# Top-2 gate and dispatch: another map from blocks of tokens to partitions

## The chip, the cores and the metric

The kernel runs on one core of one Trainium2 chip. The metric is the device time of one execution in microseconds, as the median of several runs. Before the change three runs took 239.9, 240.08 and 240.19 us, so the median is 240.08 us.

## The reference

For each of 16 x 1024 tokens there are 512 hidden values and 8 router logits. The two largest probabilities of a softmax over the logits are divided by their sum, and the token's hidden row is written twice, once times each of the two weights, the smaller first. Cut to what matters:

```python
probs = np.exp(router_logits - logits_max)
probs = probs / np.sum(probs, axis=-1, keepdims=True)
topk_indices = np.argsort(probs, axis=-1)[..., -k:]          # k = 2
topk_probs = np.take_along_axis(probs, topk_indices, axis=-1)
topk_probs = topk_probs / np.sum(topk_probs, axis=-1, keepdims=True)
x_expanded = x[:, :, np.newaxis, :].repeat(k, axis=2)
return (x_expanded * topk_probs[..., np.newaxis]).astype(np.float32)
```

x has 33.55 MB, the logits 0.52 MB and the output 67.11 MB, all float32. No two tokens depend on each other, so any token may lie in any partition as long as its row, its logits and its output agree.

## The kernel before

The 16,384 tokens are 128 partitions times 128 tokens. They are worked in two groups (`GROUPS = [65, 63]`): the first holds 65 tokens per partition, the second 63. In each group a partition holds a block of consecutive tokens: the view `(p m) d -> p m d` gives partition p the tokens p·m to p·m + m - 1 of the group. A token's row is 2 KiB, so a block is 130 KiB of x and 260 KiB of the output in the first group, 126 and 252 KiB in the second.

A group's rows are loaded into `xs` by a few transfers over all 128 partitions (`LOADS`, line 120: 2, 4, 28 and 31 tokens per partition, then 16, 16 and 31). Behind the second load the two transfers of the logits are issued (lines 125 and 126), and `top2_weights` (lines 22 to 38) finds the two largest logits of every token by a tree of max and min on VectorE; two sigmoids of their difference on ScalarE are the weights `WA`. As the exponentials' sum drops out, no softmax is formed.

Then each group is stored in pieces (`STORES`). A piece of up to 16 tokens per partition is one multiplication on VectorE (line 133), rows and weights broadcast against each other, which writes both copies. It writes into a separate buffer `osp`, or into `xs` itself over rows that are no longer needed. Where a piece goes into `osp` a second time, the multiplication is cut in two, because a part of the buffer comes free earlier. A transfer stores the piece (line 145).

All loads and all stores but the first stand in SyncE's queue, in the order in which the program gives them (`keep_in_program_order`); the first store is issued from ScalarE. SyncE waits in line: a store waits for its multiplication, and the second group's loads wait for the stores that read the buffer they overwrite.

Of the kernel before, what the change touches and what calls it, by code (L numbers as in the profile page):

```python
# [1 line left out]

# [4 lines left out]

F32 = mybir.dt.float32
ALU = mybir.AluOpType
ACTF = mybir.ActivationFunctionType  # L10
P = 128


def top2_weights(nc, WA, dlt, room, logits, E):

    tt = nc.vector.tensor_tensor
    hi, lo, n = None, None, E  # L20
    while n > 1:
        n //= 2
        if hi is None:
            a, b = logits[:, :, 0:n], logits[:, :, n : 2 * n]
            nhi, nlo = room(n), b
            tt(nhi, a, b, op=ALU.max)  # L26
            tt(nlo, a, b, op=ALU.min)  # L27
        else:
            a, b = hi[:, :, 0:n], hi[:, :, n : 2 * n]
            nhi, nlo, tmp = room(n), room(n), room(n)  # L30
            tt(tmp, lo[:, :, 0:n], lo[:, :, n : 2 * n], op=ALU.max)  # L31
            tt(nlo, a, b, op=ALU.min)  # L32
            tt(nlo, nlo, tmp, op=ALU.max)  # L33
            tt(nhi, a, b, op=ALU.max)  # L34
        hi, lo = nhi, nlo
    tt(dlt, hi[:, :, 0], lo[:, :, 0], op=ALU.subtract)  # L36
    nc.scalar.activation(WA[:, :, 0], dlt, ACTF.Sigmoid, scale=-1.0)  # L37
    nc.scalar.activation(WA[:, :, 1], dlt, ACTF.Sigmoid, scale=1.0)  # L38

GROUPS = [65, 63]

LOADS = [[2, 4, 28, 31], [16, 16, 31]]
BASE = [0, 1]

STORES = [
    [(0, 3, "osp", 0), (3, 15, "osp", 3), (18, 16, "xs", 0), (34, 15, "osp", 0), (49, 16, "xs", 33)],
    [(0, 16, "osp", 2), (16, 16, "xs", 0), (32, 15, "osp", 0), (47, 16, "xs", 32)],
]  # L50

L = 18

FREE = [3, 2]


@with_exitstack
def kernel(
    ctx: ExitStack,
    tc: tile.TileContext,  # L60
    x: bass.AP,
    router_logits: bass.AP,
    k: bass.AP,
    out: bass.AP,
):
    nc = tc.nc
    B, S, D = x.shape
    E = router_logits.shape[-1]
    N = B * S
    assert int(k) == 2 and E == 8 and N == P * sum(GROUPS)  # L70
    M = N // P

    x_v, o_v, rl_v = [], [], []
    t0 = 0
    for n in GROUPS:
        t1 = t0 + P * n
        x_v.append(
            x.rearrange("b s d -> (b s) d")[t0:t1].rearrange("(p m) d -> p m d", p=P)
        )
        o_v.append(  # L80
            out.rearrange("b s k d -> (b s) k d")[t0:t1].rearrange(
                "(p m) k d -> p m k d", p=P
            )
        )
        rl_v.append(
            router_logits.rearrange("b s e -> (b s) e")[t0:t1].rearrange(
                "(p m) e -> p m e", p=P
            )
        )
        t0 = t1  # L90

    wpool = ctx.enter_context(tc.tile_pool(name="wpool", bufs=1))
    xs = wpool.tile([P, max(GROUPS), D], F32)
    osp = wpool.tile([P, L, 2, D], F32)
    WA = wpool.tile([P, M, 2], F32)
    dlt = wpool.tile([P, M], F32)


    flat = osp.rearrange("p l k d -> p (l k d)")
    taken = [0]  # L100

    def room(n):
        o = taken[0]
        taken[0] += M * n
        return flat[:, o : o + M * n].rearrange("p (m n) -> p m n", n=n)

    logits = room(E)

    def place(where, at, n):

        if where == "osp":
            return osp[:, at : at + n]
        return xs[:, at : at + 2 * n, :].rearrange("p (r k) d -> p r k d", k=2)

    m0 = 0
    for g, G in enumerate(GROUPS):
        x0, r = BASE[g], 0
        for n in LOADS[g]:
            tc.keep_in_program_order(
                nc.sync.dma_start(xs[:, x0 + r : x0 + r + n, :], x_v[g][:, r : r + n, :])  # L120
            )
            r += n
            if g == 0 and r == 6:
                n0 = GROUPS[0]
                tc.keep_in_program_order(nc.sync.dma_start(logits[:, :n0], rl_v[0]))  # L125
                tc.keep_in_program_order(nc.sync.dma_start(logits[:, n0:], rl_v[1]))  # L126
                top2_weights(nc, WA, dlt, room, logits, E)
        assert r == G
        for r, n, where, at in STORES[g]:
            og = place(where, at, n)  # L130
            again = where == "osp" and at == 0 and r > 0
            for a, b in [(0, FREE[g]), (FREE[g], n)] if again else [(0, n)]:
                nc.vector.tensor_tensor(  # L133
                    og[:, a:b],
                    xs[:, x0 + r + a : x0 + r + b, :]
                    .unsqueeze(2)
                    .to_broadcast([P, b - a, 2, D]),
                    WA[:, m0 + r + a : m0 + r + b, :]
                    .unsqueeze(3)
                    .to_broadcast([P, b - a, 2, D]),  # L140
                    op=ALU.mult,
                )

            queue = nc.scalar if g == r == 0 else nc.sync
            tc.keep_in_program_order(queue.dma_start(o_v[g][:, r : r + n], og))  # L145
        m0 += G


# [1 line left out]
_INS = ['x', 'router_logits', 'k']  # L150
_OUTS = [((16, 1024, 2, 512), 'float32')]

_NUMBERS = {'k': 2}


# [26 lines left out]
```

## Time and profile before

| What | Value |
|---|---|
| median of three runs | 240.08 us |
| span of the profiled execution | 238.1 us |
| time of the profiled execution beside its span | not given by the page; the median is 2.0 us above the span |
| VectorE busy | 141.9 us (60%), 22 instructions |
| data moved | 101.19 MB in 2593 packets |
| mean rate over the span | 425 GB/s |
| share of the 16 DMA engines' time, SyncE's and ScalarE's queues | 97.2% and 1.5% |

The span is the time from the first to the last instruction that the hardware profiler recorded. "Busy" leaves out waiting, and the issuing of transfers. A transfer is cut into packets that 16 DMA engines move; the profile gives the time from its issue to its landing. The chain that ended last is followed back from the last instruction, at each step to what released it. In a table of stretches, a row has the stretch, its length, the busy time of each engine with the number of instructions, the clock of TensorE (which this kernel doesn't use), the DMA engines' mean busy share and the rate.

### The profile page before, as it was taken

How to read it: one execution, taken by the hardware profiler on the slowest of the kernel's cores; microseconds unless marked ns; L12 is line 12 of the kernel's file. 1: busy time of each engine (PE TensorE's matmuls, PEld its weight loads, DVE VectorE, ACT ScalarE, POOL GpSimd, SP SyncE). 2: the span in 40 equal slices, each digit the busy share in tenths (PEclk: the TensorE clock that was granted, in tenths of full speed). 3: DMA queues.
4: the chain of work that ended last, by engine and by line, in shares of the span. 5: the costliest groups of instructions: out<-in, count | busy, mean ns of one | idle time of the engine just before them, and what ended most of it. 6: DMA issues, size and time to landing. Idle time of an engine off the chain costs nothing.

```text
span 238.1 us, 105 instructions
## 1 busy us (share of the span) xinstructions
DVE 141.9 (60%) x22; ACT 1.8 (1%) x3; POOL 0.2 (0%) x4
## 2 busy tenths in 40 slices
DVE  0560499999689999100000799999406999950000
ACT  2000000000000000000000000000000000000000
POOL 0000000000000000000000000000000000000000
DMA  7979998979998999989899999898999989989894
GB/s 249 537 337 526 419 429 376 506 330 495 407 451 363 517 392 434 495 352 528 352 440 440 429 446 491 363 495 374 484 396 418 462 352 506 475 351 517 352 528 176
DMA packets 2593, 101.19 MB, mean 425 GB/s; under 512 B 289, under 2 KB 417, under 8 KB 673
## 3 DMA queue, kind: packets, MB, share of 16 engines
q1 hardware_dynamic: 2448, 99.62, 97.2%
q10 hardware_dynamic: 144, 1.57, 1.5%
q14 instruction: 1, 0.00, 0.0%
HBM read 34.08 MB, written 67.11 MB: 425 GB/s over the span
## 4 chain that ended last, share of the span: by engine, by line
DMA 48%; DVE 40%; SPq 1%; issue 0%; DVEq 0%
DVE osp L133 25%; DMA xs<-in_x_dram 25%; DMA out_dram<-osp 22%; DVE xs L133 14%; SPq L120 0%; SPq L126 0%; SPq L125 0%; SPq L145 0%; DVEq L133 0%
## 5 line engine op out<-in xcount | busy, mean ns | idle before, releaser
L133 DVE TENSOR_TENSOR osp<-xs,WA 128x3072 f32<-128x3072 f32 (+5 forms) x7 | 69.4, 9909 | 61.2 <-DMA xs<-in_x_dram 47.2
L133 DVE TENSOR_TENSOR xs<-xs,WA 128x16384 f32<-128x16384 f32 x4 | 68.9, 17224 | 0.1
L26 DVE TENSOR_TENSOR osp<-osp 128x512 f32<-128x512 f32 x1 | 0.7, 691 | 8.4 <-DMA osp<-in_router_logits_dram 8.4
L37 ACT ACT_TABLE_LOAD x1 | 1.3, 1283 | 0.7 <-PEq L163 0.7
L27 DVE TENSOR_TENSOR osp<-osp 128x512 f32<-128x512 f32 x1 | 0.7, 691 | 0.0
L31 DVE TENSOR_TENSOR osp<-osp 128x256 f32<-128x256 f32 (+1 forms) x2 | 0.7, 350 | 0.0
L32 DVE TENSOR_TENSOR osp<-osp 128x256 f32<-128x256 f32 (+1 forms) x2 | 0.7, 350 | 0.0
L34 DVE TENSOR_TENSOR osp<-osp 128x256 f32<-128x256 f32 (+1 forms) x2 | 0.7, 349 | 0.0
L33 DVE TENSOR_TENSOR osp<-osp 128x256 f32<-128x256 f32 (+1 forms) x2 | 0.7, 348 | 0.0
L37 ACT ACTIVATE WA<-dlt 128x128 f32<-128x128 f32 x1 | 0.3, 314 | 10.3 <-DVE dlt L36 10.3
L36 DVE TENSOR_TENSOR dlt<-osp 128x128 f32<-128x128 f32 x1 | 0.3, 293 | 0.0
L38 ACT ACTIVATE WA<-dlt 128x128 f32<-128x128 f32 x1 | 0.3, 298 | 0.0
L163 POOL MEMSET const-bfloat16-1.0<- 128x1 bf16 x1 | 0.1, 102 | 0.0
L163 POOL MEMSET const-uint8-127<- 128x1 uint8 x1 | 0.1, 101 | 0.0
L163 POOL MEMSET const-float32-0.0<- 128x1 f32 x1 | 0.1, 99 | 0.2 <-issue 0.2
L163 POOL MEMSET const-float32-1.0<- 128x1 f32 x1 | 0.1, 98 | 0.0
## 6 DMA issues: line engine op xcount, KB each, us to landing
out_dram<-osp SPq DMA_DIRECT2D x3, 7680.0 KB, 23.3
xs<-in_x_dram SPq DMA_DIRECT2D x2, 7936.0 KB, 41.3
xs<-in_x_dram SPq DMA_DIRECT2D x2, 4096.0 KB, 40.3
xs<-in_x_dram SPq DMA_DIRECT2D x1, 7168.0 KB, 24.4
out_dram<-osp ACTq DMA_DIRECT2D x1, 1536.0 KB, 26.9
xs<-in_x_dram SPq DMA_DIRECT2D x1, 1024.0 KB, 5.8
xs<-in_x_dram SPq DMA_DIRECT2D x1, 512.0 KB, 3.8
osp<-in_router_logits_dram SPq DMA_DIRECT2D x1, 260.0 KB, 6.0
```

Of the source, the lines that this page charges most:

```text
L26: tt(nhi, a, b, op=ALU.max)
L27: tt(nlo, a, b, op=ALU.min)
L31: tt(tmp, lo[:, :, 0:n], lo[:, :, n : 2 * n], op=ALU.max)
L32: tt(nlo, a, b, op=ALU.min)
L33: tt(nlo, nlo, tmp, op=ALU.max)
L34: tt(nhi, a, b, op=ALU.max)
L36: tt(dlt, hi[:, :, 0], lo[:, :, 0], op=ALU.subtract)
L37: nc.scalar.activation(WA[:, :, 0], dlt, ACTF.Sigmoid, scale=-1.0)
L38: nc.scalar.activation(WA[:, :, 1], dlt, ACTF.Sigmoid, scale=1.0)
L133: nc.vector.tensor_tensor(og[:, a:b], xs[:, x0 + r + a : x0 + r + b, :] .unsqueeze(2) .to_broadcast([P, b - a, 2, D]), WA[:, m0 + r + a : ...
L163: nc = _bacc.Bacc("TRN2", target_bir_lowering=False, num_devices=1)
```

## The change

Loads, logits and stores all go by another map. Each group's 128 blocks are numbered in four quarters of 32: block 32j + a is the a-th of quarter j. Before, block p lay in partition p. After, block 32j + a lies in partition 4a + j, so that four neighbouring partitions hold one block from each quarter, and the next four hold the blocks next to these.

On the DRAM side a transfer is then described by 32 x 4 pieces with two strides, in place of 128 with one; on the partitions' side it is still 128. A piece is as long as before. In the built program every instruction stands where it stood: the order on VectorE, ScalarE and SyncE and the shapes on VectorE are the same, and the 18 transfers differ only in their DRAM side, such as 32 x 4 x 15360 for a store that had 128 x 15360.

```diff
     for n in GROUPS:
         t1 = t0 + P * n
         x_v.append(
-            x.rearrange("b s d -> (b s) d")[t0:t1].rearrange("(p m) d -> p m d", p=P)
+            x.rearrange("b s d -> (b s) d")[t0:t1].rearrange(
+                "(j a m) d -> a j m d", j=4, m=n
+            )
         )
         o_v.append(
             out.rearrange("b s k d -> (b s) k d")[t0:t1].rearrange(
-                "(p m) k d -> p m k d", p=P
+                "(j a m) k d -> a j m k d", j=4, m=n
             )
         )
         rl_v.append(
             router_logits.rearrange("b s e -> (b s) e")[t0:t1].rearrange(
-                "(p m) e -> p m e", p=P
+                "(j a m) e -> a j m e", j=4, m=n
             )
         )
...
-                nc.sync.dma_start(xs[:, x0 + r : x0 + r + n, :], x_v[g][:, r : r + n, :])
+                nc.sync.dma_start(xs[:, x0 + r : x0 + r + n, :], x_v[g][:, :, r : r + n, :])
...
-            tc.keep_in_program_order(queue.dma_start(o_v[g][:, r : r + n], og))
+            tc.keep_in_program_order(queue.dma_start(o_v[g][:, :, r : r + n], og))
```

## The prediction

> **What bounds the kernel now.** I read the page first for who is busy: busy times, the DMA queues, the chain that ended last.
>
> ```profile
> span 238.1 us, 105 instructions
> DVE 141.9 (60%) x22; ACT 1.8 (1%) x3; POOL 0.2 (0%) x4
> DMA packets 2593, 101.19 MB, mean 425 GB/s; under 512 B 289, under 2 KB 417, under 8 KB 673
> ...
> q1 hardware_dynamic: 2448, 99.62, 97.2%
> q10 hardware_dynamic: 144, 1.57, 1.5%
> ...
> HBM read 34.08 MB, written 67.11 MB: 425 GB/s over the span
> ...
> DMA 48%; DVE 40%; SPq 1%; issue 0%; DVEq 0%
> ```
>
> VectorE is busy for 60% of the span, the packets of SyncE's queue (q1) and ScalarE's queue (q10) for 97.2% + 1.5% = 98.7% of what 16 DMA engines have. The chain's 40% of DVE is no counter-evidence: the chain passes through whichever work was late locally, while the transfers never pause. The second view, waits, says the same: VectorE waits for transfers, 47.2 us for loads and 13.5 us for stores to free buffers.
>
> ```profile
> DVE osp L133 <- DMA xs<-in_x_dram: 47.2, 2, 36.4
> DVE osp L133 <- DMA out_dram<-osp: 13.5, 2, 11.1
> ```
>
> The third view cuts the span into stretches (length; busy us of DVE, ACT, POOL; clock; DMA share; GB/s).
>
> ```profile
> core 0: us, DVE busy (x) ACT busy (x) POOL busy (x), PEclk, DMA share, GB/s
> 0.00:4.00 4.00, 0.00 (x0) 1.28 (x1) 0.20 (x4) 1.00 0.57 166
> 4.00:24.00 20.00, 7.18 (x12) 0.51 (x2) 0.00 (x0) 1.00 1.09 458
> 24.00:28.00 4.00, 1.01 (x1) 0.00 (x0) 0.00 (x0) 1.00 0.82 352
> 28.00:154.00 126.00, 87.08 (x7) 0.00 (x0) 0.00 (x0) 1.00 1.01 436
> 154.00:164.00 10.00, 10.00 (x1) 0.00 (x0) 0.00 (x0) 1.00 0.96 413
> 164.00:214.00 50.00, 36.64 (x4) 0.00 (x0) 0.00 (x0) 1.00 0.99 431
> 214.00:234.00 20.00, 0.00 (x0) 0.00 (x0) 0.00 (x0) 1.00 1.00 433
> 234.00:238.10 4.10, 0.00 (x0) 0.00 (x0) 0.00 (x0) 1.00 0.41 176
> 30.00:230.00 200.00, 131.72 (x10) 0.00 (x0) 0.00 (x0) 1.00 1.00 433
> ```
>
> A share above 1 (1.09) shows that a packet is booked whole where it begins, so only long stretches are exact. From 30 to 230 us the rate is 433 GB/s with all 16 engines full. It is 433 in 214:234, where only stores run and VectorE is idle, and 436 in 28:154, where loads, stores and VectorE overlap. A rate that does not care for direction or for neighbours looks like a limit of the engines themselves, not of the memory behind them. So the time is bytes over rate plus ends: 101.19 MB / 433 GB/s = 233.7 us, and the span is 238.1. The other 4.4 us are the start (166 GB/s up to 4 us), the tail (176 after 234) and two weak stretches, 24:28 and 154:164. The page gives the profiled execution no time of its own beside the span; the median of the three runs, 240.08, is 2.0 us above it, and I carry those 2.0 us over. The working formula is **time = 101.19 MB / rate + 6.4 us**.
>
> **The change part by part.** Nothing is added to or taken from VectorE or ScalarE: the same eleven multiplications, the same weights, the same order of issue on every queue. The bytes do not change, nor does the longest piece of contiguous DRAM, since each partition still holds one block of 65 (or 63) consecutive tokens; so I expect the same 128 data packets per transfer and 2593 in all. Three things do change.
>
> (a) *The DRAM side of each of the 18 transfers has one level more*, 32 x 4 x run in place of 128 x run. What that costs the issuing queue is not in the trace; the nearest rows are the issues as they are.
>
> ```profile
> L120 SPq DMA_DIRECT2D xs<-in_x_dram x7: 328/449/927, 0.7 to 123.2; - x7
> L145 SPq DMA_DIRECT2D out_dram<-osp x4: 332/338/348, 43.2 to 194.5; - x4
> L145 ACTq DMA_DIRECT2D out_dram<-osp x1: 366/366/366, 16.3 to 16.3; - x1
> 0.72 0.37 SPq L120
> ...
> 1.15 0.43 SPq L120
> ```
>
> Only the first issue, 0.37 us from 0.72 us on, stands before any data. At worst it becomes the longest load issue seen, 0.93 us: +0.56 us. At best it costs nothing, and I know of no reason for a gain; I take +0.05, since the row nearest to it (0.43 us) differs by that. The four issues behind it are covered by the data ahead of them: 512 KB take 1.2 us at 433 GB/s against 0.43 us per issue. The later issues are covered by the queue:
>
> ```profile
> out_dram<-osp SPq DMA_DIRECT2D x3, 7680.0 KB, 23.3
> xs<-in_x_dram SPq DMA_DIRECT2D x2, 4096.0 KB, 40.3
> xs<-in_x_dram SPq DMA_DIRECT2D x1, 512.0 KB, 3.8
> out_dram<-osp ACTq DMA_DIRECT2D x1, 1536.0 KB, 26.9
> ```
>
> A store of 7680 KB lands 23.3 us after its issue and needs 7.86 MB / 433 GB/s = 18.2 us, so about 5.1 us of older work are still ahead of it. An issue that is 0.6 us longer, or a landing that one engine delays by a packet, doesn't empty the queue. ScalarE's one store holds up nobody: nothing stands behind it on ScalarE, and it lands 26.9 us later, among other transfers. Were the cover gone, every one of the eight large stores would show its issue, 8 x 0.34 = 2.7 us.
>
> (b) *Which tokens lie in which partition.* Partition 4a + j now holds block 32j + a. Loads, logits and stores use the same map, so weights and rows stay together; it costs no instruction. Zero.
>
> (c) *Which DRAM addresses are touched together.* A block is 65 x 2 KiB = 130 KiB of x and 260 KiB of out (126 and 252 in the second group). If an engine takes four neighbouring partitions one after another, then before, engines side by side were 520 KiB apart in x and an engine stepped by 130 KiB; after, they are 130 KiB apart and each engine steps by 32 x 130 KiB = 4160 KiB (8320 in out). The best this can do is to remove the two weak stretches: (433 - 352) x 4 / 433 = 0.75 us and (433 - 413) x 10 / 433 = 0.46 us, together -1.2 us; the start can't be read as an address effect, since the first transfer's latency stands in it. The worst within the rows is that all traffic runs as in those stretches: at 413 GB/s 245.0 + 6.4 = 251.4 us, at 352 GB/s 287.5 + 6.4 = 293.9 us. I take 0, because the rate is flat at 431 to 436 over patterns as unlike as 520 KiB loads, 1040 KiB stores and mixtures of both: what shows no dependence on the pattern in nine tenths of the span should not gain or lose by another.
>
> Sum: 240.08 + 0.05 + 0 = **240.1 us**.
>
> The Trainium skill has a rule that speaks against (c): "DMA: Bandwidth & Descriptors", section "Latency and other measured facts", gives copies whose partitions lie 4 or 8 MiB apart in DRAM 103 GB/s per direction against 214 at full rate, and the full rate again once 4 KiB are added to the pitch. Neighbouring partitions here come to 4 MiB + 64 KiB and 8 MiB + 128 KiB, so by the rule's padded row nothing happens (240.1), and by its unpadded row an estimate of 101.19 / (433 x 103 / 214) + 6.4 = 492 us. No trace of this case has such a pitch yet.
>
> **The rivals.**
>
> *The weak stretches go* (faster). They are address collisions of the old spacing and the new one has none: 240.1 - 1.2 = 238.9 us, or 239.4 if only the larger goes. For it: both fall into times when loads and a store are in flight together. Against it: 28:154 has such mixtures too and runs at 436.
>
> *The new addresses collide* (slower). Sixteen streams 130 KiB apart, each jumping 4 MiB + 64 KiB, meet in the same part of the memory for a time. Its price starts at one more pair of weak stretches, +1.2 us = 241.3 us, and reaches 251.4 us if all traffic runs at 413 GB/s; it decides once the rate in 30:230 falls below 432 GB/s (0.2% of 233.7 us is 0.5 us). For it: 352 GB/s shows that a rate below the engines' can occur. Against it: that lasts for some 4 of 238 us. The skill's pitch rule, above, is its strong form.
>
> *The engines are shared out differently* (much slower). With 32 x 4 on one side and 128 on the other the transfer need not be dealt to the 16 engines in the old way. If they fall into pairs that must go through the same place, or if half of them carry all of it, the rate is 433 / 2 and the time 101.19 / 0.2165 + 6.4 = 473.8 us. For it: the shares of 98.7% leave no spare engine, so any unevenness is paid in full: an engine with a tenth more bytes adds 23 us. Against it: 32 and 128 are both multiples of 16, so an even deal exists. The Trainium skill has both halves. "DMA: Bandwidth & Descriptors", section "Why a DMA increments its semaphore by 16 and not by 1", lets the number of engines be the largest up to 16 that divides the slowest dimension of both sides, which gives 16 here. "SBUF — State Buffer", section "Door 1: The DMA port swizzle", has partitions 32 apart share a port, so that an engine with eight consecutive partitions would share ports with another; whether this shape is dealt so, neither says. No run here shows it.
>
> *The change does nothing that can be seen* is the forecast itself: addresses move, but the limit is not there.
>
> **How the numbers follow.** Forecast 0.56 (its own range 239.5 to 240.9: the +0.56 us of the first issue, and the spread of the runs, 239.9 to 240.19, doubled on either side); weak stretches gone 0.15; collisions 0.11; a different deal of engines 0.18. The last two get much weight for things without a row: the trace holds no transfer with unequal sides. Two runs of this kernel differ by up to 0.12%, so 0.2% (0.5 us) is about what can be told from no change. Faster by more than that: 0.15 + 0.04 from the forecast's lower edge = 0.19. Within it: 0.44. Slower: 0.18 + 0.11 + 0.08 from the forecast's upper edge = 0.37. The range leaves out the deal of engines (0.18) and the far end of the collisions (0.02): it goes from 238.8, both weak stretches gone, to 251, all traffic at 413 GB/s.
>
> **What the profile after would show.** For (a): the issue rows of loads and stores at 0.33 to 0.45 us, the first load of 512 KB landing after about 3.8 us; longer ones and an equal span would say that the queue covers them. For (c): 30:230 at 433 GB/s with share 1.00, 2593 packets and the same sizes. The first rival shows 24:28 and 154:164 at 433. Collisions show a share of 1.00 with fewer GB/s. A different deal shows either shares far below 1.00 (engines without work) or a share of 1.00 at some 217 GB/s (engines in each other's way), and VectorE's waits for DMA several times as long. The forecast is wrong if the rate in 30:230 is not 433 by more than 1 GB/s.

## The result and the profile after

The changed kernel takes 241.97 us as the median of 7 runs (240.81 to 243.96), beside 240.03 us (239.9 to 240.79, 7 runs) of the kernel before: a ratio of 1.0082, with a 95% interval of 1.0059 to 1.0104. A second series on another occasion gave 241.66 us (240.36 to 243.42, 12 runs) beside 240.09 us, a ratio of 1.0062 (1.0032 to 1.0093). So the change makes the kernel slower by 0.6 to 0.8%. As telling as the median is the spread: 12 of these 19 runs lie above 241.2 us, of the kernel before 6 of 106 over all series.

The profiled execution took 242.84 us, one of the longest, with a span of 241.0 us. First its page, to be held against the page of before:

```profile
span 241.0 us, 105 instructions
DMA packets 2592, 101.19 MB, mean 420 GB/s; under 512 B 288, under 2 KB 416, under 8 KB 672
q1 hardware_dynamic: 2448, 99.62, 96.1%
```

The bytes and the packets are those of before, but for one packet outside SyncE's and ScalarE's queues. Then the stretches of the changed kernel, columns as in the prediction:

```profile
0.00:4.00 4.00, 0.00 (x0) 1.28 (x1) 0.20 (x4) 1.00 0.43 109
24.00:28.00 4.00, 0.00 (x0) 0.00 (x0) 0.00 (x0) 1.00 0.87 365
154.00:164.00 10.00, 10.00 (x1) 0.00 (x0) 0.00 (x0) 1.00 0.98 419
234.00:241.00 7.00, 0.00 (x0) 0.00 (x0) 0.00 (x0) 1.00 0.37 159
30.00:230.00 200.00, 133.12 (x10) 0.00 (x0) 0.00 (x0) 1.00 1.00 434
```

Between 30 and 230 us nothing has changed: 434 GB/s against 433. The weak stretches are still there. What is different is at the two ends: 109 GB/s against 166 up to 4 us, and a tail that lasts to 241.0 instead of 238.1. The chain of work that ended last dates the loss. Columns are start, length and what; before first, then after:

```profile
26.99 16.17 DVE osp L133
132.71 17.24 DVE osp L133
149.96 30.50 DMA out_dram<-osp
180.48 14.04 DVE osp L133
```
```profile
28.38 16.17 DVE osp L135
134.50 17.24 DVE osp L135
151.75 31.62 DMA out_dram<-osp
183.39 14.04 DVE osp L135
```

The same three multiplications start 1.39, 1.79 and 2.91 us later, and the end is 2.9 us later. So the loss comes in steps: 1.39 us by the first large load, 0.4 us by the next waits, and 1.1 us more by the wait for a store, whose piece of the chain took 31.62 us instead of 30.50; its packets stand behind those of the last load. These are points at which work waits for *all* engines of a transfer.

The first step has a plain part, the issues. Rows of the loads, the stores and ScalarE's store, and the first piece of the chain:

```profile
L122 SPq DMA_DIRECT2D xs<-in_x_dram x7: 535/657/1159, 0.7 to 124.7; - x7
L147 SPq DMA_DIRECT2D out_dram<-osp x4: 539/567/605, 44.6 to 197.4; - x4
L147 ACTq DMA_DIRECT2D out_dram<-osp x1: 622/622/622, 16.9 to 16.9; - x1
0.73 0.67 SPq L122
```

Every issue is longer by 0.2 to 0.3 us: 0.67 against 0.37 for the first, medians of 0.66 against 0.45 for loads. How many packets began before 2.1 us shows what that does to the first data, before and then after:

```profile
q1 hardware_dynamic: 15, 0.06, 28.7%
```
```profile
DMA packets 0, 0.00 MB, mean 0 GB/s; under 512 B 0, under 2 KB 0, under 8 KB 0
```

By the packet records the first begins at 1.74 us before and at 2.17 after: 0.43 us.

The last step is uneven engines. Of the packets that begin after 236.2 us, the kernel before has only the 16 small ones that report the end of a transfer; the changed one has two of 64 KB more, 0.13 MB:

```profile
q1 hardware_dynamic: 16, 0.00, 0.5%
```
```profile
q1 hardware_dynamic: 18, 0.13, 6.5%
```

By the records, before, the last data packets of all engines end between 236.33 and 236.85 us. After, 14 engines end by 237.36, the other two at 238.83 and 239.77. Each engine has its fixed share (8 of a large load's 128 packets in the records, a late engine's too), so the kernel ends with the last of them. The records do not name the engine; followed from each packet to the one that begins where it ends, the latest engine's slow packets are these (start in us, bytes, ns taken, ns usual):

```
21.7   57344   2574   2116
24.7   57344   2858   2116
46.7   63488   2828   2342
160.1  63488   3594   2342
```

All four are load packets just ahead of a store's packets on that engine. Together they cost 2.9 us, which is what the profiled run lost. On the other engines the second cost about 0.45 us, and the others next to nothing.

### The profile page after: what moved, and what is told of

It is laid out like the page before. It is cut to its first block, busy times and chain, and to the rows that moved or that the text cites. A ratio compares the mean times of both kernels' runs of the same rounds, so it can differ in the third digit from the quotient of the medians.

```text
span 241.0 us, 105 instructions
## 1 busy us (share of the span) xinstructions
DVE 141.9 (59%) x22; ACT 1.8 (1%) x3; POOL 0.2 (0%) x4
## 3 DMA queue, kind: packets, MB, share of 16 engines
q10 hardware_dynamic: 144, 1.57, 1.5%
## 4 chain that ended last, share of the span: by engine, by line
DMA 48%; DVE 39%; SPq 1%; issue 0%; DVEq 0%
DMA xs<-in_x_dram 25%; DVE osp L135 25%; DMA out_dram<-osp 23%; DVE xs L135 14%; SPq L122 1%; SPq L128 0%; SPq L127 0%; SPq L147 0%; DVEq L135 0%
```

## The experiments

All medians stand beside runs of the kernel before on the same occasion and chip. There were three such occasions: one for the first four kernels, one for the repeat of the changed kernel, the added transfer and the moved store, and one for the last four kernels. "Late runs" are those above 241.2 us.

**The start, and the rest.** Two kernels split the change. In the first, only the first two loads and the logits go by the new map:

```diff
+            new = g == 0 and r < 6
+            xr = x_v[g][:, :, r : r + n, :] if new else x_old[g][:, r : r + n, :]
...
-            tc.keep_in_program_order(queue.dma_start(o_v[g][:, :, r : r + n], og))
+            tc.keep_in_program_order(queue.dma_start(o_old[g][:, r : r + n], og))
```

> Only the first two loads (6 tokens per partition) and both logits transfers go by the new map; the large loads and all stores by the old one. So the weights are not those of the stored rows: the work is the same, its result another. Theory START (the longer issue delays the first packet by 0.4 to 0.5 us, and the uneven start of the engines grows into the late tail): about 242.0 us, with engines that end 2 to 3 us apart. Theory LOADS (single engines fall behind in the large loads by the new addresses) and theory STORES (the same for stores): 240.5 us, the start's 0.45 us alone, engines ending within 0.6 us.

Measured: 240.76 us (240.22 to 242.83, 12 runs) against 240.04, ratio 1.0036 (1.0008 to 1.0063); 4 late runs. In the second it is the other way round, `new = not (g == 0 and r < 6)`, logits by the old views and stores by the new:

> The complement: the first two loads and the logits by the old map, the three large and two middle loads and all stores by the new one, so weights and rows again don't belong together. START: 240.1 us, since the first packet comes as early as before. LOADS and STORES: 241.3 to 241.7 us, the whole of the loss but the 0.45 us of the start.

Measured: 240.34 us (239.77 to 242.49, 12 runs), ratio 1.0013 (0.9984 to 1.0042); 3 late runs. No theory got its numbers. The first kernel's quickest run is 0.5 us above that of the kernel before (239.71), which is the later start; the second's is level. But late runs occur in both. Neither has as many as the whole change, though with 12 runs each the counts don't tell them apart: the first kernel's interval reaches into both of the changed kernel's. The profiled run of the first kernel took 242.83 us and had one late engine with slow packets in the same places, although its large loads and all its stores use the old addresses: by the records its slow packets lie at 21.7, 24.6, 46.6 and 160.0 us, took 2456, 2833, 2800 and 3644 ns, and the engine ended at 239.77 us. So an engine falls behind without any new address in the large transfers.

**Loads alone, stores alone.** In the changed kernel the stores keep the old view, and in the kernel before the stores get the new one:

```diff
-                "(j a m) k d -> a j m k d", j=4, m=n
+                "(p m) k d -> p m k d", p=P
```

> All loads and the logits by the new map, the stores by the old one: the rows are right but written to other places of the output than the reference's. START and LOADS: 241.8 to 242.2 us, as the changed kernel. STORES: 240.5 us, the start alone.

Measured: 240.62 us (240.29 to 242.62, 12 runs), ratio 1.0031 (1.0006 to 1.0057); 3 late runs.

> Stores by the new map, all loads and the logits by the old one: rows are written to other places than the reference's. START and LOADS: 240.0 us, no difference, although each store's issue takes 0.56 us in place of 0.34. STORES: 241.5 us.

Measured: 240.24 us (239.88 to 241.45, 12 runs), ratio 1.0006 (0.9985 to 1.0026); 1 late run. The loads carry the later start (lowest 240.29), the stores cost nothing that can be told. Again the late runs are not in one part. No single culprit among the transfers is found: START, LOADS and STORES each predicted 241.3 to 242.2 us for some kernel here, and no median reached it. START has its size against it, and the late runs of the second kernel, whose start is the old one.

**Does a lag grow?** The four slow packets suggested that an engine which is late becomes later. To give two engines a known lag, a transfer of two pieces of 28 KB, DRAM to DRAM, was added to the kernel before, once behind the logits and once behind the last load:

```diff
+    scratch = nc.dram_tensor("scratch", [2, 14 * D], F32).ap()
+    spare = x_v[1][126:128, 0:14, :].rearrange("p m d -> p (m d)")
...
+                tc.keep_in_program_order(nc.sync.dma_start(scratch, spare))
                 top2_weights(nc, WA, dlt, room, logits, E)
```

> The kernel before with one more small transfer behind the logits: two pieces of 28 KB, DRAM to DRAM, which are to give two engines alone 1.06 us more work each by 10 us. Theory GROW (an engine that is late reads its last load packets while the others write already, and loses more each time): these two engines are 1.1 us late at 10 us, about 2 at 28 us and 3.5 at the end; 242.5 to 243.5 us, in all runs. Theory FIXED (a lag stays what it is): 1.1 us late at the end too, 240.6 to 241.1 us.

> The same small transfer, but behind the last load, so that no load follows in which the two late engines could fall further behind. GROW and FIXED both: 240.6 to 241.1 us, the two engines ending 1.1 us after the others. If it takes as long as with the early one, the place in the sequence doesn't matter and GROW falls.

Measured: 242.54 us with the early one (242.35 to 242.64, 4 runs), ratio 1.0092 (1.0063 to 1.0122), and 241.11 us with the late one (240.87 to 241.51, 10 runs), ratio 1.0029 (1.0011 to 1.0048), both against 240.09. The same added work costs 2.45 us early and 1.02 us late. FIXED falls. The growth that GROW expected is there, though 2.4 us at the end in place of 3.5; the reason that GROW gives for it is not shown by this. By the records of the early kernel two engines end at 239.25 and 239.27 us, 2.4 us behind the other 14 (236.86 at the latest), and their slow packets are those of the changed kernel: 2926 and 3061 ns at 24.7 us, 3478 and 3314 ns at 159.7 and 159.9 us. The early kernel's four runs agree within 0.3 us, and its time is that of the changed kernel's late runs.

**The weak stretch at 24 us.** The first store goes to SyncE's queue, behind the loads:

```diff
-            queue = nc.scalar if g == r == 0 else nc.sync
+            queue = nc.sync
```

> The kernel before with its first store issued from SyncE's queue, in which it stands behind both of the first group's large loads, so that no store runs beside the loads at 19 to 27 us. Theory MIX (the weak stretch at 24 to 28 us comes from writes beside reads): the stretch is gone, 239.5 us, and an engine's lag can no longer grow there, so that runs above 240.5 us become rare. Theory ADDRESS (the stretch belongs to the load's addresses): unchanged, 240.0 us, with a weak stretch at the same place.

Measured: 240.45 us (240.17 to 240.82, 12 runs) against 240.09, ratio 1.001 (0.9996 to 1.0024); no late run. MIX was right that the stretch at 24 us would go and that late runs become rare, and wrong on the gain:

```profile
24.00:28.00 4.00, 2.94 (x1) 0.00 (x0) 0.00 (x0) 1.00 1.17 508
40.00:44.00 4.00, 3.96 (x2) 0.00 (x0) 0.00 (x0) 1.00 0.86 260
154.00:164.00 10.00, 10.00 (x1) 0.00 (x0) 0.00 (x0) 1.00 0.98 419
```

The stretch at 24:28 is gone and a deeper one has come at 40:44 (260 GB/s, where the kernel before has 508; some of that is packets that began ahead of it), just before the stores now begin. This weak stretch goes with the first stores, not with the addresses of the load that is in flight. The other one, at 154:164, stayed (419 GB/s).

MIX's reason, writes beside reads, does not fit the new stretch. By the records each engine's last load packet there began between 40.53 and 40.98 us and took 3.0 to 3.7 us, where 2.34 is usual, and the first store packet of any engine began only at 43.93 us, when all of them were past 2.34 us. So load packets ahead of a store can be slow before any store packet has begun; why is open.

**What leaves an engine behind.** In the kernel before, the first store's packets (ScalarE's queue, q10) arrive when nearly all engines are just ending their sixth packet of the large load. Packets of q10 that began from 20 to 22 us, before and after:

```profile
q10 hardware_dynamic: 15, 0.18, 21.6%
```
```profile
q10 hardware_dynamic: 2, 0.02, 2.9%
```

Before, 15 engines take a store packet there and one goes on. After, two do, and 14 go on to the seventh load packet: the store comes later, as the start is later and its own issue longer (0.62 against 0.37 us), and it arrives among the late edge of the engines' packet ends. The two take a store packet while the others read, and read while the others have gone on to stores. They are the two that end late, and they were behind already: their first packets of the large load, at 8 us, began 0.54 and 0.27 us after the median engine's. A third engine, 0.42 us behind there, went on to its seventh load packet and ended with the others. By this theory the moment of the store's arrival decides. It was moved by a copy on ScalarE ahead of the first store, in place over part of the piece, on the kernel before with n = 256 and 1024 elements, and on the changed kernel with 1024:

```diff
+            if g == r == 0:
+                part = og[:, 0].rearrange("p k d -> p (k d)")[:, 0:1024]
+                nc.scalar.activation(part, part, ACTF.Copy)
             queue = nc.scalar if g == r == 0 else nc.sync
```

> The kernel before with one copy of 256 elements on ScalarE, in place over the first piece, ahead of the first store, which so comes some 0.4 to 0.5 us later; nothing else changes. Theory PHASE (an engine whose 16 neighbours have gone on to their seventh load packet when the store's packets arrive, while it takes a store packet first, is left behind and then falls back further): the arrival moves from the early edge of the engines' packet ends into their late part, some engines are left behind, and runs above 241.2 us become frequent (a third or more; in the kernel before 5 of 71); median 240.2 to 241.5. Theory NOT PHASE: the late store is covered, 240.05 us, runs as before.

Measured: 240.46 us (240.0 to 242.43, 12 runs) against 240.03, ratio 1.0016 (0.9992 to 1.0041); 2 late runs, fewer than the third that was expected. In its profile 7 engines take the store packet at 20 to 22 us and 9 go on.

> The same with 1024 elements, which makes the store some 1.0 us later, behind the packet ends of all engines, so that all take the seventh load packet first. PHASE: 240.0 us, and hardly a run above 240.6: quicker than with the smaller delay. NOT PHASE: 240.05 us, as the kernel before; a cost of the added work itself would make it slower than the smaller delay.

Measured: 240.12 us (239.78 to 242.42, 12 runs), ratio 1.0002 (0.9981 to 1.0023); 1 late run. The longer delay is not slower than the shorter one. The two intervals overlap, so this pair alone would not settle it.

> The changed kernel with the copy of 1024 elements ahead of its first store, about 1.0 us later than it is there. PHASE: the slow runs go, 240.5 us with hardly one above 241.2 (in the changed kernel 12 of 19): an added wait makes it quicker by 1.2 us. NOT PHASE: 241.7 us as without it, or more.

Measured: 240.29 us (240.13 to 241.63, 12 runs), ratio 1.0009 (0.9992 to 1.0027); 1 late run, where the changed kernel without the copy had 7 of 12 (1.0062, 1.0032 to 1.0093). The intervals don't meet. The two kernels ran on different occasions and chips, so each is compared with its own runs of the kernel before: 0.26 us above them with the copy, 1.57 us without. A copy of 1.06 us, with a wait of the store for it, makes the changed kernel 1.3 us faster. The rows are the copy, and the packets that begin from 22 to 24 us:

```profile
L148 ACT ACTIVATE osp<-osp 128x1024 f32<-128x1024 f32 x1 | 1.1, 1056 | 3.4 <-DVE osp L135 3.4
```
```profile
q1 hardware_dynamic: 16, 0.92, 127.7%
q10 hardware_dynamic: 16, 0.20, 23.0%
```

Now all 16 engines take their first store packet in this stretch, after the same seventh load packet, and by the records all end between 236.67 and 237.19 us.

**The changed kernel with the store behind the loads**, the edit of the weak-stretch experiment made on the changed kernel:

> The changed kernel with its first store issued from SyncE, behind the large loads, so that no store packet comes between load packets. PHASE: no engine can be left behind there; 240.9 us (the 240.45 of the same edit on the kernel before, and 0.45 for the later start), hardly a run above 241.4. If the new addresses or the later issues make engines late by themselves: 241.7 us with the same wide spread.

Measured: 240.71 us (240.42 to 241.58, 12 runs), ratio 1.0023 (1.0008 to 1.0039); 2 late runs. It is 0.26 us above the same edit on the kernel before, within what the later start costs. The new addresses add nothing that can be told beside it.

**What the profiles leave open.** The two kernels that move the changed kernel's first store speak for PHASE by their medians; the profiles do so less. In those of the second split kernel and of the stores kernel, too, only 2 and 3 engines took a store packet at 20 to 22 us, and no engine ended after 237.52 us. In the late run of the first split kernel it was 10. What the two late runs share is an engine that was behind before any store came: 0.54 us behind the median engine at its first packet of the large load in the changed kernel, 0.62 in the first split kernel. In the other profiles, but for that of the early added transfer (0.93), the latest engine was at most 0.50 us behind there. So an uneven start of the engines is a rival, alone or together with the store's moment. The copy comes after that start and can't change it, and with it the late runs went from 7 of 12 to 1 of 12; but no run settles how much belongs to each.

The repeat of the changed kernel, whose numbers stand in the first section, was expected so:

> The changed kernel once more, beside the other three on one chip, for the spread of its runs. From the runs so far: its quickest runs some 0.5 us above the quickest of the kernel before (the later start alone), others up to 3.5 us above; median 241 to 242 us. If the new addresses cost something in every run, the quickest are 0.9 us or more above.

Its quickest run is 0.57 us above the quickest of before (240.36 against 239.79), its profiled one took 240.53 us: there 7 engines took the store packet at 20 to 22 us, and all ended between 236.78 and 237.49 us. Where no engine falls behind, the later start remains. No kernel here is faster than the one before.

## Why the prediction was right or wrong

The time lies in the range (238.8 to 251) and above the forecast's own range (239.5 to 240.9). The likeliest case, no change within 0.2%, did not come; slower had 0.37. None of the three rivals describes what happened. That the time lies in the range is luck: above 240.9 us the range was made for colliding addresses, at 241.3 us and more, and none were found.

- **Bytes over rate.** Right on the rate: 434 GB/s in 30:230, the same packets and the same weak stretches. Wrong on the ends: the 6.4 us were carried over as a constant, while the formula holds only if the 16 engines end together. The prediction's own test ("wrong if the rate in 30:230 is not 433 by more than 1 GB/s") could not see this loss.
- **(a), the first issue.** The mechanism was right, the size was not: +0.05 us was taken, between 0 and +0.56. The issue grew by 0.30 us, the first packet came 0.43 us later, and the kernels with a new first load had quickest runs 0.4 to 0.7 us above those of before (0.9 in the first series, of 7 runs). The later issues were covered as said; SyncE's longer ones left the rate at 434.
- **(a), "ScalarE's one store holds up nobody".** This is the step that failed, as far as the runs show. The store stands in nobody's way on its queue, and it was costed at nothing for that reason. But its packets come between the load packets on the engines, and when they come matters. With a copy of 1.06 us ahead of the store, the changed kernel is 0.26 us above the kernel before in place of 1.57: some 1.3 us of the change's 1.6 to 1.9 us hang on this moment. With the store behind the loads the late runs are 2 of 12.
- **(c), the addresses.** 0 was right as far as the runs tell: the pitch of 4 MiB + 64 KiB (4 MiB - 64 KiB in the second group) runs at 434 GB/s. The distances of 520 and 130 KiB between engines side by side don't follow, since they give an engine four partitions and by the records each takes 8 of a transfer's 128 packets; the sum doesn't use them. By the Trainium skill's rule on DRAM pitch ("DMA: Bandwidth & Descriptors", "Latency and other measured facts") the trace agrees with the padded row; no run here has an unpadded pitch.
- **The weak stretches** were read as possible address collisions. The one at 24 us goes with the first stores: when the first store moved, the stretch moved with it. The one at 154:164 stayed, and its reason is open.
- **A different deal of the engines** did not come: 434 GB/s and share 1.00 in 30:230 mean that all 16 engines have work and none halves another's rate. The Trainium skill's rule on the number of engines ("DMA: Bandwidth & Descriptors", "Why a DMA increments its semaphore by 16 and not by 1"), by which 32 and 128 give 16, agrees with that.

What stays open: why late engines are so much more frequent with the whole change (12 of 19) than with any part of it (1 to 4 of 12). Moving the store cures most of it; the counts of the parts are too small to divide the cause between the later and uneven start, the longer issue of the store and the loads' addresses. That the lag grows *because* an engine reads while others write is not shown: it is inferred from where the slow packets stand, and with the first store behind the loads load packets were slow before any store packet had begun. Shown is that the same lag costs 1.4 us more ahead of the load-to-store changes than behind them. And 1 run in 12 was still late with the longer delay, so the store's moment is not the only way to fall behind.

## What to carry to other kernels

Where transfers are cut into fixed shares for 16 engines, a full average rate is not yet the time: look at when the first and the last engine end, and at the spread of the runs, because the last engine sets the end, and an engine's lag can grow. A transfer that is off every critical path can still matter by the moment at which its packets come between those of another queue. A second stride on the DRAM side isn't free: it lengthened each issue here by 0.2 to 0.3 us, which showed where no data was in flight yet: ahead of the first packet.

## What the runs showed of the hardware that had not been expected

- Packets of 1.06 us more, given to two engines ahead of the large loads, had become a lag of 2.4 us at the end, and cost 2.45 us; given behind the last load, they cost 1.02 us.
- An added wait made a kernel faster: 241.66 to 240.29 us with a copy of 1.06 us ahead of the first store (1.57 and 0.26 us above the kernel before, each on its own occasion).
- The rate fell where stores first began beside or behind loads: 352 to 365 GB/s at 24:28, and 260 GB/s at 40:44 when the first store came there. There the load packets ahead of the stores took 3.0 to 3.7 us in place of 2.34, and were past 2.34 before any store packet had begun.
- With 32 x 4 pieces on the DRAM side, an issue on SyncE took 0.54 to 1.16 us (0.33 to 0.93 before) and on ScalarE 0.62 us (0.37).
